# A planner's rule for TensorE's transposes, one modelled wire for two kinds of transfers, and new due times, in a hybrid attention and MLP layer

## The chip, the core and the metric

The kernel runs on one core of one Trainium2 chip. The metric is the device time of one execution in microseconds. A core has five engines that run side by side, each through its own list of instructions in order: TensorE (PE in the profile, with its weight loads apart as PEld), VectorE (DVE), ScalarE (ACT), GpSimd (POOL) and SyncE (SP, which here only starts transfers).

## The reference, cut to what matters

One layer (DEPTH = 1) on 512 tokens of width 1024, all in float32:

```python
hn = rms_norm(h, ln_mix); z = hn @ w_in
q1, q2, k1, k2, va, qf, kf, vf, fg, qc, kc, vc = split(z)
o_a = diff_attention(q1, q2, k1, k2, va, ...)   # 4 heads, two softmax maps each
o_b = forgetting_attention(qf, kf, vf, log_f)   # 6 heads, causal
o_c = chunk_attention(qc, kc, vc, rel_bias)     # 6 heads
h = h + concat(o_a, o_b, o_c) @ w_out
h = h + conv_gated_mlp(rms_norm(h, ln_ffn), w_up, conv_w, conv_b, w_down)   # d_ff = 2816
gate = sigmoid(rms_norm(h, ln_ple) @ w_ple_gate)
h = h + (p @ w_ple_proj) * gate
```

All queries and keys are normalised per head (64 wide) before the scores.

## The kernel before

Every large product is made of three passes: each operand is split into a high part (`hi`, written as fp32r) and the rest (`lo`), and `mm3` (L479) adds hi x hi, hi x lo and lo x hi into one PSUM bank. Splitting costs one ACT copy and one DVE subtraction for each tile of weights or activations (`load_w`, L407; `split`, L463). For a part of the weights the subtraction is instead done by POOL, or by a transfer that adds (`pool.dma_start` with `accum_op`, L428).

The work falls into stages. `first_products` (L584) multiplies the first eight pieces of x, k = 0 to 7, as they are loaded, with the first block of `w_in`: 8 x 12 matmuls of 384 columns. The next block is "A0b", 262 columns, whose four unit groups are called in1_0 to in1_3 (four weight tiles, made by `in_w(1)`). Then come the projections in2 to in9 (`in_unit`, `project`), the preparation of queries and keys ("A0a" and the like, `qk_cols`, L757), scores (`scores`, L846), the transposing of probabilities (`prob_cols`, L870), values (`values`, L898), and the output projection (out0, out1). Transposes run on TensorE against an identity matrix, in fp32, into one PSUM bank for four at a time (`feature_cols` L674, `prob_cols`, `split_cols` L493, `forget_cumsum` L770). 16 heads take 10 transposes of probabilities each, in three groups (kb = 0: 4, kb = 1: 3, the rest: 3). The MLP and the gate follow from L1222 on.

**The order is made by a planner.** While the program is built, the engines' calls are not issued but recorded as `Op`s in a `Plan` (L100), with what they read and write. There are two plans: the first holds all up to the end of the attention part (emitted at L1100), the second the rest (L1108 to L1944). `price` (L160) gives each operation a duration (a transpose 0.109 us, an fp32r matmul 0.0004556 us a column and 0.001), a lag, and for transfers the bytes (`move`). `due` (L201) gives each TensorE operation a due time: the sum of the durations of TensorE's operations ahead of it in program order, plus what `SHIFT` (L53) says for its group; other operations are due early enough for the ones that wait for them. A group is the name that `PLAN[-1].group` had when the operation was recorded: "in1_1", "A0s01", or at first "first". Groups that `SHIFT` does not name are not moved.

`solve` (L212) then walks through time. Again and again it takes the engine that can act first, and of the operations that are ready there the one due first (L237). On TensorE an operation counts as ready only `SURE` after its inputs (L236). For transfers it keeps two clocks, `wire["sp"]` for those from SP (0.37 MB a us) and `wire["pool"]` for those from POOL (0.105 MB a us); at most 8 of a queue are open at once (L250 to L256). The order that comes out is the order in which `emit` issues the instructions; on the chip each engine keeps to it and waits by semaphores. The planner's times are not used in any other way.

In the second plan a further list of tasks (`Task`, L1252) sets the program order of the MLP; its `dl` and `trial` are not touched.

Of the kernel before, what the change touches and what calls it, by code (L numbers as in the profile page):

```python
# [41 lines left out]
for _i in range(3):  # L42
# [5 lines left out]
AHEAD = 2  # L48
# [2 lines left out]


SHIFT = {  # L53
# [14 lines left out]
}  # L68


# [29 lines left out]
class Plan:  # L100
# [59 lines left out]
    def price(self, op):  # L160
        e, k = op.eng.name, op.k
        n = self.width(op.outs[0])
        cols = sum(1 for v in op.ins if self.width(v) == 1) - (op.name == "reciprocal")
        acc = "accum_out" in k
        op.move = 0
        if e == "pe":
            if op.name == "transpose":
                op.busy = 0.109
            else:
                op.busy = n * 0.0004556 + 0.001 if op.ins[0].dtype == F32R else n * 0.0017  # L170
            op.lag = 0.165
        elif e == "act":
            op.busy, op.lag = 0.06 + n * 0.00088 + (0.18 + 0.04 * cols if acc else 0.09 * cols), 0.1
            f = k.get("func", op.a[2] if len(op.a) > 2 else None)
            if f in (AF.Silu, AF.Sigmoid) and f not in self.loaded:
                self.loaded.add(f)
                op.busy += 1.3
        elif e == "dve":
            n = max([n] + [self.width(v) for v in op.ins])
            op.busy, op.lag = 0.07 + n * 0.001045 * (1 + (op.name == "tensor_tensor_scan")) + 0.06 * cols, 0.083  # L180
        elif op.name == "dma_start":
            op.move = n * 4 * op.outs[0].shape[0]
            op.busy, op.lag = (0.9 if e == "pool" else 0.45), 0.0
        elif op.name == "tensor_tensor":
            op.busy, op.lag = ((0.42 + n * 0.155) if k["op"] == ALU.pow else (0.1 + n * 0.0024)), 0.04
        elif op.name == "memset":
            op.busy, op.lag = 0.05 + n * 0.0009, 0.04
        else:
            op.busy, op.lag = 0.08 + n * 0.00103 + (0.12 if n > 8 else 0.2) * cols, 0.04
        op.busy *= self.SPARE.get(e, 1.0)  # L190
        here = [v for v in op.ins if v.tensor.space != bass.MemoryType.PSUM]
        op.port = e == "pool" and not op.move or e == "dve" and (
            len(here) == len(op.ins) and (op.name == "tensor_scalar" or op.name in ("tensor_tensor", "scalar_tensor_tensor")))

    LONG = 0.6
    HW, SW, AT_ONCE = 0.37e6, 0.105e6, 8
    SURE, AHEAD, MUCH, WAIT = 0.15, 1.0, 2.0, 0.6
    SPARE = {"act": 1.02, "dve": 1.02, "pool": 1.05}
    ENGINES = ("dve", "pe", "act", "pool", "sp")

# [11 lines left out]
    def solve(self):  # L212
        clock = dict(self.clock)
        free = {e: [] for e in self.ENGINES}
        for op in self.ops:
            op.left, op.at = len(op.deps), op.ready + self.LEAD[op.eng.name]
            if not op.left:
                free[op.eng.name].append(op)
        wire, out, order = {"sp": 0.0, "pool": 0.0}, {"sp": [], "pool": []}, []
        held = {"dve": 0.0, "pool": 0.0}  # L220
        other = {"dve": "pool", "pool": "dve"}
        when = lambda q: max(q.at, held[other[q.eng.name]] + (self.late if q.eng.name == "pool" else 0.0)) if q.port else q.at
# [1 line left out]
        while True:  # L224
# [8 lines left out]
            t, e = best  # L233
            can = [q for q in free[e] if when(q) <= t]
            if e == "pe":
                can = [q for q in can if q.at + self.SURE <= t] or can  # L236
            op = min(can, key=rank)  # L237
            if e not in ("pe", "sp"):
                soon = [q for q in free[e] if t < when(q) < t + op.busy * self.AHEAD and q.dl < op.dl - self.MUCH]
                if soon:  # L240
                    u = min(soon, key=rank)
                    short = [q for q in can if t + q.busy <= when(u) + 0.05]
                    if short:
                        op = min(short, key=rank)
                    elif when(u) - t < self.WAIT:
                        op = u
            free[e].remove(op)
            t0 = max(clock[e], when(op))
            busy = op.busy * (1.85 if e == "pe" and t0 < 8.6 else 1.0)
            if op.move:  # L250
                done = out[e]
                if len(done) >= self.AT_ONCE:
                    t0 = max(t0, done[-self.AT_ONCE])
                wire[e] = max(t0 + 2.0, wire[e]) + op.move / (self.HW if e == "sp" else self.SW)
                op.end = wire[e] + 0.6
                done.append(op.end)  # L256
            else:
                op.end = t0 + busy + op.lag
# [32 lines left out]
def kernel(ctx: ExitStack, tc: tile.TileContext, x, xt0, xt, pt_in, small, g_ffn_in, bias_c,  # L291
# [813 lines left out]
    for q in ("hi", "lo"):  # L1105
        pi.tile([P, 768], F32R, tag=f"w{q}", bufs=W[q])
        MORE_RAW.append(pi.again(f"w{q}", W[q], F32))
    PLAN.append(Plan(first.last, (), first.mem, first.last["dve"] + 0.6, 0.1))  # L1108

    CONV = 10  # L1110

# [106 lines left out]
    def add_h(n, j, acc):  # L1218
        for b, c in ADDS[j]:
            dve.tensor_tensor(out=hblk(b, n, c), in0=hblk(b, n, c), in1=pv(acc), op=ALU.add)  # L1220

    ple_cols()  # L1222
    for n, k in ((0, 0), (0, 1), (1, 0)):
        ple_load(n, k)
    last_out(0)
    ffn_norm(0)
    last_out(1)
    ffn_norm(1)
    last_out(2)
    ffn_norm(2)  # L1230
    for t in range(NT):
        ple_unit(0, t)
    ffn_cols(0)
    last_out(3)
    ple_load(1, 1)
    ffn_norm(3)
    ffn_cols(1)
    for t in range(2):
        ple_unit(1, t)
    mp.turn["conv"] += 2  # L1240
    for t in range(2, NT):
        ple_unit(1, t)

    SLACK, URGENT = 0.8, 3.0

# [6 lines left out]
    class Task:  # L1252


        def __init__(self, kind, parts, do, deps=(), makes=(), uses=()):
            self.kind, self.parts, self.do, self.deps = kind, parts, do, [d for d in deps if d is not None]
            self.makes, self.end, self.dl, self.next, self.after = makes, None, 1e9, [], []
            for s in (*makes, *uses):
                s.users.append(self)
            for s in uses:  # L1260
# [10 lines left out]
    COUNT = {"raw": NRAW, "hi": NHI, "conv": CONV, "pin": 1, "left": 3, "x": 3, "z": 2, "s": 2, "t": 3, "o": 1}  # L1271
    TURN = {tag: [] for tag in COUNT}
    TASKS = []


    def DV(n):
# [2 lines left out]
    def AC(n):  # L1279
        return "act", 0.2 + n * 0.00083  # L1280
# [225 lines left out]
    def up_plain(f):  # L1506
# [11 lines left out]
            return do  # L1518

        for g in range(2):  # L1520
            pe_task(36, some(g, range(6)), [more()], (), [us[g]])
            yield
        last = []
        more()
        for g in range(2):
            last.append([pe_task(12, some(g, range(6, KD)), [ws[2]], (), (), [us[g]])])
# [3 lines left out]
    def up_seven(f):  # L1530
# [5 lines left out]
        own = lambda odd, h_: [[T[(2 * i + odd) // 4][:, (2 * i + odd) % 4, h_ * H : (h_ + 1) * H] for T in (Th, Tl)] for i in range(4)]  # L1536

        def prod(o, j, right, first, deps=()):
            def do():
                if first:  # L1540
                    v[o] = bank(slots[o].tag, f"s{o}{f}")
# [51 lines left out]
    class Down:  # L1593
# [6 lines left out]
        def product(self, what, phs=None, last=True):  # L1600

            j = tuple(RIGHT).index(what)
            li, ri, an, begins = PRODUCTS[j]
            assert ri == RIGHT[what]
            for ph in phs or self.phs:
# [64 lines left out]
    def first(f, g, a):  # L1670
        def do():
# [4 lines left out]
            for k in range(KD):  # L1676
                mm3(U[c][:, cs], *first_w[f][1](g, k), Th[k // 4][:, k % 4, cs], Tl[k // 4][:, k % 4, cs], k == 0, k == KD - 1)

        if a == 0:
            us[f, g] = Slot("zs"[g])  # L1680
        return pe_task(24, do, [first_w[f][0][g], first_w[f][0][2]], FORM if a else (), [us[f, g]] if a == 0 else (), [us[f, g]] if a else ())

    def cols2(t, g):

        v, s, sm = {}, Slot("t"), Slot("pin")

        def tr():
# [97 lines left out]
    COLS3 = {}  # L1785

    def cols3(t, g):
        v, s = {}, Slot("t")

        def tr():  # L1790
# [42 lines left out]

    def gate(n, t, c0, c1):
        c = slice(n * S + c0, n * S + c1)
        v, s = {}, Slot("z")
        pps, ys = Slot("conv"), Slot("conv")

# [18 lines left out]
        for k in range(KD):  # L1857
            p = pe_task(6 * (c1 - c0) / S, lambda k=k: do(k), [wg[n][k]], [COLS3[t, g] for g in range(2)], [s] if k == 0 else (), () if k == 0 else [s])
            if (n, t) == (0, 0) and k in (2, 5):
                cols3(2 + k // 4, 1)  # L1860
        GATE_ENDS.append(Task("do", [AC(c1 - c0), DV(c1 - c0), DV(c1 - c0)], end, [p, load_, STATS[t]], [ys], [s, pps]))

    class Rest:
# [64 lines left out]
    while order:  # L1928
# [5 lines left out]
        else:  # L1934
# [4 lines left out]
            late = min((q for x, q in tr if x <= first_at + SLACK), key=lambda q: q.dl)  # L1939
            q = late if late.dl < q.dl - URGENT else q  # L1940
        _, q.end, clock = trial(q)
        q.do()
        order.remove(q)
    PLAN.pop().emit()  # L1944
# [63 lines left out]
```

## Time and profile before

| | |
|---|---|
| time, median of 3 runs | 709.53 us (709.39 to 709.59) |
| time of the profiled execution | 709.35 us |
| its span, first to last instruction | 707.2 us |
| mean granted TensorE clock | 0.998 |
| busy: PE, PEld | 698.1 us (99%), 631.3 us (89%) |
| busy: DVE, ACT, POOL | 538.4 us (76%), 392.6 us (56%), 259.5 us (37%) |
| moved | 83.22 MB, mean 118 GB/s |

The share of busy time is the time in which an engine had an instruction at work, over the span. The profile's lines name an instruction by engine, operation and "out<-in" with the program's names of tiles: `t<-ident,e` is a transpose of probabilities into a bank with tag t, `z<-whi,Th` the hi x hi pass of a projection. A line number is nearly always 325, that of the helper which issues. Rows of waits give total time, how often, and the longest; rows of the timeline give start, duration, engine and instruction, and how many of them were merged ("x4"). TensorE's matmuls overlap in the records, so that the distance from one start to the next, not the duration, is what one takes.

### The profile page before, as it was taken

How to read it: one execution, taken by the hardware profiler on the slowest of the kernel's cores; microseconds unless marked ns; L12 is line 12 of the kernel's file. 1: busy time of each engine (PE TensorE's matmuls, PEld its weight loads, DVE VectorE, ACT ScalarE, POOL GpSimd, SP SyncE). 2: the span in 40 equal slices, each digit the busy share in tenths (PEclk: the TensorE clock that was granted, in tenths of full speed). 3: DMA queues.
4: the chain of work that ended last, by engine and by line, in shares of the span. 5: the costliest groups of instructions: out<-in, count | busy, mean ns of one | idle time of the engine just before them, and what ended most of it. 6: DMA issues, size and time to landing. Idle time of an engine off the chain costs nothing.

```text
span 707.2 us, 11820 instructions
## 1 busy us (share of the span) xinstructions
PE 698.1 (99%) x4204; PEld 631.3 (89%) x4204; DVE 538.4 (76%) x1090; ACT 392.6 (56%) x745; POOL 259.5 (37%) x355
## 2 busy tenths in 40 slices
PE   7999999999999999999999999999999999999997
PEld 7999999999999888898888899889998888999886
DVE  7688899787887765879889477994689869777722
ACT  6657776675676663846564355463545444545711
POOL 3687686757664641212011142113410004353300
PEclk9999999999999999999999999999999999999999
DMA  9543553313211163745445124832263232124431
GB/s 328 201 104 91 125 136 115 104 53 105 97 46 61 61 149 108 229 148 137 162 127 145 65 90 127 201 104 63 72 193 121 87 115 79 59 66 148 143 90 52
DMA packets 36950, 83.22 MB, mean 118 GB/s; under 512 B 4214, under 2 KB 6262, under 8 KB 36892
## 3 DMA queue, kind: packets, MB, share of 16 engines
q1 hardware_dynamic: 32844, 73.52, 32.1%
q0 software_dynamic: 3760, 8.66, 6.9%
q8 instruction: 33, 0.54, 0.3%
q10 hardware_dynamic: 288, 0.30, 0.1%
q14 instruction: 25, 0.20, 0.1%
HBM read 74.19 MB, written 4.21 MB: 111 GB/s over the span
## 4 chain that ended last, share of the span: by engine, by line
PE 97%; POOL 1%; DMA 0%; DVE 0%; issue 0%; ACT 0%; POOLq 0%
PE z L325 50%; PE s L325 24%; PE t L325 15%; PE o L325 7%; DMA zn<-in_w_in_dram 0%; POOL e L325 0%; POOL rs L325 0%; POOL wlo L325 0%; DVE conv L325 0%; DVE oall L325 0%; ACT otmp L325 0%; ACT whi L325 0%; DVE zn L325 0%; ACT conv L325 0%; ACT ptc L325 0%
## 5 line engine op out<-in xcount | busy, mean ns | idle before, releaser
L325 ACT CAST whi<-wraw 128x768 fp32r<-128x768 f32 (+2 forms) x132 | 99.4, 768 | 59.0 <-PE t L325 18.1
L325 PE MATMUL z<-whi,Th 128*128 128x384 f32 (+2 forms) x356 | 123.2, 355 | 4.5 <-ACT whi L325 4.4
L325 PE MATMUL z<-wlo,Th 128*128 128x384 f32 (+2 forms) x356 | 121.9, 352 | 0.0
L325 PE MATMUL z<-whi,Tl 128*128 128x384 f32 (+2 forms) x356 | 121.6, 351 | 0.0
L325 DVE TENSOR_TENSOR wlo<-wraw,whi 128x768 fp32r<-128x768 f32 (+2 forms) x114 | 100.7, 893 | 24.9 <-ACT whi L325 24.6
L325 PEld LDWEIGHTS z<-whi,Th 128*128 128x128 f32 x356 | 67.4, 190 | 8.9 <-ACT whi L325 4.4
L325 PEld LDWEIGHTS z<-whi,Tl 128*128 128x128 f32 x356 | 67.1, 189 | 4.2
L325 PEld LDWEIGHTS z<-wlo,Th 128*128 128x128 f32 x356 | 67.2, 189 | 3.4
L325 POOL TENSOR_TENSOR wraw<-wraw,wraw 128x768 f32<-128x768 f32 (+1 forms) x14 | 23.9, 1706 | 120.8 <-DVE conv L325 75.4
L325 PE MATMUL z<-Th,whi 128*128 128x512 f32 (+1 forms) x180 | 66.3, 368 | 0.1
L325 PE MATMUL z<-Tl,whi 128*128 128x512 f32 (+1 forms) x180 | 66.2, 368 | 0.0
L325 PE MATMUL z<-Th,wlo 128*128 128x512 f32 (+1 forms) x180 | 66.1, 367 | 0.0
L325 PE MATMUL s<-Tl,whi 128*128 128x512 f32 (+1 forms) x180 | 65.1, 367 | 0.0
L325 PE MATMUL s<-Th,wlo 128*128 128x512 f32 (+1 forms) x180 | 65.0, 367 | 0.0
L325 PE MATMUL s<-Th,whi 128*128 128x512 f32 (+1 forms) x180 | 64.8, 367 | 0.0
L325 ACT ACTIVATE e<-e,st 128x128 f32<-128x128 f32 (+3 forms) x80 | 44.6, 559 | 16.6 <-DVE st L325 16.2
L325 POOL TENSOR_TENSOR rs<-rs,nhalf 128x4 f32<-128x4 f32 x40 | 43.1, 1088 | 4.9 <-DVE rs L325 1.4
L325 DVE SCALAR_TENSOR_TENSOR conv<-z,cols,conv 128x511 f32<-128x511 f32 (+1 forms) x38 | 28.4, 748 | 15.7 <-ACT conv L325 15.0
L325 PEld LDWEIGHTS s<-Th,wlo 128*128 128x128 f32 x180 | 33.8, 188 | 6.2
L325 PEld LDWEIGHTS z<-Th,whi 128*128 128x128 f32 x180 | 33.8, 188 | 6.2 <-issue 0.3
L325 PEld LDWEIGHTS s<-Tl,whi 128*128 128x128 f32 x180 | 33.8, 188 | 6.2
L325 PEld LDWEIGHTS z<-Th,wlo 128*128 128x128 f32 x180 | 33.8, 188 | 6.1
(351 smaller groups left out, 1884.1 us busy)
## 6 DMA issues: line engine op xcount, KB each, us to landing
wraw<-in_w_up_dram SPq DMA_DIRECT2D x33, 384.0 KB, 3.8
wraw<-in_w_in_dram SPq DMA_DIRECT2D x28, 384.0 KB, 3.5
wraw<-in_w_down_dram SPq DMA_DIRECT2D x17, 384.0 KB, 3.0
whi_again<-in_w_up_dram SPq DMA_DIRECT2D x12, 384.0 KB, 3.7
wraw<-in_w_out_dram SPq DMA_DIRECT2D x16, 256.0 KB, 2.8
wraw<-in_w_up_dram SPq DMA_DIRECT2D x13, 256.0 KB, 3.4
wlo<-wraw POOLq DMA_DIRECT2D x7, 384.0 KB, 4.8
wraw<-in_w_ple_gate_dram SPq DMA_DIRECT2D x10, 256.0 KB, 3.1
```

What stands on the lines that cost most here:

```text
L325: ins = getattr(self.eng, op)(*a, **k)
```

## The change

It touches the planner and its table of due times; no instruction is added to or removed from the kernel.

- `op.turns` marks transposes. On TensorE, when the most urgent ready operation is of the other kind than the last one issued, `solve` looks for ready operations of the same kind due less than `STICK` = 2.0 us later. At transposes it goes on with those. At matmuls it goes on with those if fewer than two transposes are at hand, or if the first of these matmuls is due less than 1.0 us later.
- The first matmul behind a transpose that stood alone is charged 0.08 us more in the planner's clock.
- `SURE` goes from 0.15 to 0.1.
- `wire` is one clock for transfers of both queues; the two rates stay.
- `SHIFT` is new for nearly all groups of the first plan. "first" has an entry now.
- In the second plan each group gets a name of its own (`called`, `GROUP`, and `PLAN[-1].group = q.group` where tasks are issued). `SHIFT` has an entry for none of them; its first group is called "rest" so that the entry of "first" does not reach it.

```diff
 SHIFT = {
-    "in1_1": 0.4, "in1_2": -4.5, "A0a": 0.1, "in1_3": -3.6, "in2_0": -0.9, "in2_1": 1, "A0b": 23.2, "in2_2": -4.2,
-    "A0s01": -13.3, "A0s02": -12.2, "in2_3": -2.1, "fc": 21.6, "in3_0": 3.4, "A0p0": -8.9, "A0v0": 8.1, "in3_1": -1,
...
+    "first": -11.4, "in1_0": -0.3, "in1_1": -25, "in1_2": -2.7, "A0a": -6.5, "in1_3": -12.1, "in2_0": -5.9,
+    "in2_1": 19.7, "A0b": -17.1, "in2_2": -18.9, "A0s01": -25, "A0s02": -5.9, "in2_3": -4.1, "fc": 0.8, "in3_0": 4.7,
...
-        op.move = 0
+        op.move, op.turns = 0, op.name == "transpose"
...
-    LONG = 0.6
+    LONG, STICK = 0.6, 2.0
...
-    SURE, AHEAD, MUCH, WAIT = 0.15, 1.0, 2.0, 0.6
+    SURE, AHEAD, MUCH, WAIT = 0.1, 1.0, 2.0, 0.6
...
-        wire, out, order = {"sp": 0.0, "pool": 0.0}, {"sp": [], "pool": []}, []
+        wire, out, order = 0.0, {"sp": [], "pool": []}, []
+        turns, alone = False, False
...
             op = min(can, key=rank)
+            if e == "pe" and op.turns != turns:
+                same = [q for q in can if q.turns == turns and q.dl < op.dl + self.STICK]
+                if same and (turns or sum(q.turns and q.dl < op.dl + self.STICK for q in can) < 2 or min(q.dl for q in same) < op.dl + self.STICK / 2):
+                    op = min(same, key=rank)
...
             busy = op.busy * (1.85 if e == "pe" and t0 < 8.6 else 1.0)
+            if e == "pe":
+                busy += 0.08 * (alone and not op.turns)
+                turns, alone = op.turns, op.turns and not turns
...
-                wire[e] = max(t0 + 2.0, wire[e]) + op.move / (self.HW if e == "sp" else self.SW)
-                op.end = wire[e] + 0.6
+                wire = max(t0 + 2.0, wire) + op.move / (self.HW if e == "sp" else self.SW)
+                op.end = wire + 0.6
...
     PLAN.append(Plan(first.last, (), first.mem, first.last["dve"] + 0.6, 0.1))
+    PLAN[-1].group = "rest"
...
+    def called(name, do, *a):
+        PLAN[-1].group = name
+        do(*a)
```

More of the change, by code (lines that the diff above doesn't have):

```diff
@@ L1224 @@
         ple_load(n, k)
[L1225 to L1230, printed above, removed]
+    called("last_out_0", last_out, 0)
+    called("ffn_norm_0", ffn_norm, 0)
+    called("last_out_1", last_out, 1)
+    called("ffn_norm_1", ffn_norm, 1)
+    called("last_out_2", last_out, 2)
+    called("ffn_norm_2", ffn_norm, 2)
     for t in range(NT):
-        ple_unit(0, t)
-    ffn_cols(0)
-    last_out(3)
+        called(f"ple_unit_0_{t}", ple_unit, 0, t)
+    called("ffn_cols_0", ffn_cols, 0)
+    called("last_out_3", last_out, 3)
     ple_load(1, 1)
-    ffn_norm(3)
-    ffn_cols(1)
+    called("ffn_norm_3", ffn_norm, 3)
+    called("ffn_cols_1", ffn_cols, 1)
     for t in range(2):
-        ple_unit(1, t)
+        called(f"ple_unit_1_{t}", ple_unit, 1, t)
     mp.turn["conv"] += 2
     for t in range(2, NT):
-        ple_unit(1, t)
+        called(f"ple_unit_1_{t}", ple_unit, 1, t)
     SLACK, URGENT = 0.8, 3.0
@@ L1257, in __init__ @@
             self.makes, self.end, self.dl, self.next, self.after = makes, None, 1e9, [], []
+            self.group = GROUP[0]
             for s in (*makes, *uses):
@@ L1273 @@
     TASKS = []
+    GROUP = ["first"]
     def DV(n):
@@ L1520, in up_plain @@
         for g in range(2):
+            GROUP[0] = f"u{f}_{g}"
             pe_task(36, some(g, range(6)), [more()], (), [us[g]])
@@ L1523, in up_plain @@
         last = []
+        GROUP[0] = f"u{f}_2"
         more()
@@ L1538, in prod @@
         def prod(o, j, right, first, deps=()):
+            GROUP[0] = f"s{f}_{j}"
             def do():
@@ L1602, in product @@
             j = tuple(RIGHT).index(what)
+            GROUP[0] = f"{self.name}_{what}"
             li, ri, an, begins = PRODUCTS[j]
@@ L1677, in do @@
                 mm3(U[c][:, cs], *first_w[f][1](g, k), Th[k // 4][:, k % 4, cs], Tl[k // 4][:, k % 4, cs], k == 0, k == KD - 1)
+        GROUP[0] = f"u{f}_{g}{a}"
         if a == 0:
@@ L1683, in cols2 @@
     def cols2(t, g):
+        GROUP[0] = f"x{t}{g}"
         v, s, sm = {}, Slot("t"), Slot("pin")
@@ L1787, in cols3 @@
     def cols3(t, g):
+        GROUP[0] = f"h{t}{g}"
         v, s = {}, Slot("t")
@@ L1835, in gate @@
         c = slice(n * S + c0, n * S + c1)
+        GROUP[0] = f"g{n}{t}_{c0}"
         v, s = {}, Slot("z")
@@ L1860, in gate @@
                 cols3(2 + k // 4, 1)
+                GROUP[0] = f"g00_{k}"
         GATE_ENDS.append(Task("do", [AC(c1 - c0), DV(c1 - c0), DV(c1 - c0)], end, [p, load_, STATS[t]], [ys], [s, pps]))
@@ L1941 @@
         _, q.end, clock = trial(q)
+        PLAN[-1].group = q.group
         q.do()
```

23 rows, old and new, of the table SHIFT are left out of this document.

## The prediction

> **What bounds the kernel now.** I read the page first (busy shares, chain of waits), then the windows by stage, then what TensorE's weight loads wait for, then the timeline of TensorE around its transposes.
>
> ```profile
> span 707.2 us, 11820 instructions
> PE 698.1 (99%) x4204; PEld 631.3 (89%) x4204; DVE 538.4 (76%) x1090; ACT 392.6 (56%) x745; POOL 259.5 (37%) x355
> PE 97%; POOL 1%; DMA 0%; DVE 0%; issue 0%; ACT 0%; POOLq 0%
> ```
>
> TensorE is busy 99% of the span and is 97% of the chain that ended last. The other engines matter only where TensorE stands still for them. The windows, one row a stage, say where that can be:
>
> ```profile
> 0.00:9.00 9.00, 4.62 (x15) 4.61 (x16) 4.81 (x11) 4.59 (x8) 5.80 (x15) 1.00 0.82 264
> 36.00:70.00 34.00, 33.91 (x225) 32.18 (x224) 28.75 (x90) 22.00 (x58) 27.28 (x45) 1.00 0.36 96
> 360.00:700.00 340.00, 340.00 (x2028) 300.05 (x2027) 248.83 (x354) 160.81 (x235) 75.47 (x67) 1.00 0.37 109
> 700.00:708.00 8.00, 2.98 (x25) 2.77 (x24) 1.70 (x4) 0.95 (x2) 0.00 (x0) 0.81 0.19 66
> ```
>
> The columns are stretch, length, busy time of PE, weight loads, DVE, ACT and POOL, then clock, DMA share and GB/s. TensorE starts 4.38 us into the span (4.62 busy of the first 9.00) and ends at 702.98, 4.2 us before the end. The MLP stretch, 360 to 700, is full. A busy PE hides short gaps here, because the end of a matmul is modelled and one record overlaps the next; so the gaps are read from the weight loads, which stand ahead of every matmul. All their waits between 36 and 250 us, the attention stage (total, times, longest):
>
> ```profile
> PEld s L325 <- DVE st L325: 0.9, 3, 0.4
> PEld t L325 <- DVE zn L325: 0.6, 2, 0.4
> PEld t L325 <- issue: 0.5, 2, 0.3
> PEld z L325 <- DVE zn L325: 0.4, 2, 0.2
> PEld t L325 <- ACT pth L325: 0.4, 1, 0.4
> PEld t L325 <- POOL e L325: 0.4, 1, 0.4
> PEld s L325 <- POOL k L325: 0.3, 1, 0.3
> PEld z L325 <- issue: 0.3, 1, 0.3
> PEld t L325 <- DVE ptl L325: 0.3, 1, 0.3
> PEld s L325 <- issue: 0.2, 1, 0.2
> PEld o L325 <- ACT pth L325: 0.2, 1, 0.2
> PEld o L325 <- DVE oall L325: 0.2, 1, 0.2
> PEld o L325 <- DVE ptl L325: 0.2, 1, 0.2
> ```
>
> They sum to 4.9 us in 18 waits of 0.2 to 0.4 us. From 250 us to the end the same view has one row, equal to the "z <- issue" row above: 0.3 us. Two things follow. All that a better order can win is about 4.9 + 0.3 us, 0.7% of the span. And no releaser in the list is a DMA: TensorE nowhere waits for a load once it runs.
>
> **The change part by part. First, transposes in runs.** The new planner charges 0.08 us more when one transpose stands alone between matmuls (`alone`), and keeps transposes together (`STICK`). What a lone one costs is in the timeline (start, duration):
>
> ```profile
> 102.74 0.28 PE L325 MATMUL s<-kl,q 128*128 128x256 f32 x1
> 102.85 0.28 PE L325 MATMUL s<-k,q 128*128 128x256 f32 x1
> ...
> 103.62 0.60 PE L325 MATMUL t<-ident,e 128*128 128x128 f32 x4
> 103.97 0.36 PE L325 MATMUL s<-k,q 128*128 128x256 f32 x1
> 104.18 0.27 PE L325 MATMUL t<-ident,e 128*128 128x128 f32 x1
> 104.20 0.37 PE L325 MATMUL s<-kl,q 128*128 128x256 f32 x1
> 104.41 0.27 PE L325 MATMUL t<-ident,e 128*128 128x128 f32 x1
> ```
>
> Go by starts, not durations. A 256-column matmul between matmuls takes 0.11 us (102.74 to 102.85; 0.118 is the median of its 1590 cases in the same view). The run of four with the matmul behind it takes 103.62 to 104.18, 0.56 us; less 0.118 leaves 0.44, or 0.111 a transpose. The lone one with its matmul takes 104.18 to 104.41, 0.23; less 0.118 leaves 0.112. The matmul behind a lone transpose does look 0.08 us slow (0.21 against 0.118), but it starts only 0.02 after the transpose instead of 0.11: the same time, put down to the other record. Over all runs I find 113.5 ns for a lone one, 222.6 for a pair, 441 for four: about 109 each and 4.5 a run.
>
> There are 312 transposes in 130 runs, 67 of them lone, the first and the last of these:
>
> ```profile
> 32.94 0.27 PE L325 MATMUL t<-ident,zn 128*128 128x128 f32 x1
> 307.52 0.27 PE L325 MATMUL t<-ident,conv 128*128 128x128 f32 x1
> ```
>
> If all 67 pair up, 34 runs of 4.5 ns go: 0.15 us. If they join longer runs, 67 go: 0.3 us. If none joins, nothing. By the planner's own 0.08 it would be 5.4 us, which the rows above exclude. I take **-0.15 us**.
>
> [...]
>
> ```profile
> L325 PE MATMUL t<-ident,e x160: 269/272/328, 55.6 to 265.0; 128*128 128x128 f32 x160
> 652.57 1.04 PE L325 MATMUL t<-ident,h 128*128 128x128 f32 x8
> ```
>
> **Second, where runs cost.** In `solve`, when a transpose is the most urgent ready operation and TensorE is at matmuls, it is now passed over as long as a ready matmul is due within 1.0 us behind it (within 2.0 if fewer than two transposes are at hand). Once in a run, matmuls up to 2.0 us more urgent wait for the rest of it. TensorE loses nothing itself, it only swaps. But behind a transpose come the ACT copy and the DVE subtraction of its columns, and TensorE's scores or values wait for both. In the window from 36 to 70 DVE is busy 28.75 of 34 us (85%) and POOL 27.28 (80%): a chain that starts 1 us later finds little room to catch up. Its bounds: nothing where other matmuls fill in (they did for all but 18 waits), and one more wait of 0.2 to 0.4 us for each held group. `SURE`, from 0.15 to 0.1, points the same way: operations are taken with 0.05 us less margin, at most 0.05 on each of 18 waits, 0.9 us.
>
> **Third, the due times.** Nearly every group of the attention part is moved, by up to 25 us, and "first" for the first time. This draws the order of 36 to 250 us anew. It removes no matmul and adds none, so its worth lies between all waits gone (-4.9) and, where it goes badly, a second set of the same size (+4.9). The trace shows these waits as single chains that came 0.2 to 0.4 us late with five different causes, no one cause that a new order would cure. I take **0**: about as many waits elsewhere.
>
> **Fourth, the start.** "in1_1" is moved by -25, "first" by -11.4. By the planner's prices the 96 matmuls of `first_products` run from 4.5 in steps of 0.176 to 21.4, the 24 of in1_0 to 24.3; so in1_1 is due at -0.7, and step k=4 of the first products at 4.5 - 11.4 + 4 x 2.11 = 1.5. The four loads of the A0b weights, which stood behind all x and W loads, now go out ahead of x's k=4. The rows on this:
>
> ```profile
> 4.67 0.43 SPq L325 DMA_DIRECT2D bias<-in_xt_dram  x1
> 10.12 0.33 SPq L325 DMA_DIRECT2D wraw<-in_w_in_dram  x1
> wraw<-in_w_in_dram SPq DMA_DIRECT2D x4, 262.0 KB, 5.6
> 10.13 0.73 ACT L325 ACTIVATE Th<-bias,cols 128x512 fp32r<-128x512 f32 x1 [0.58 <-DMA bias<-in_xt_dram]
> 14.95 0.63 ACT L325 CAST whi<-wraw 128x524 fp32r<-128x524 f32 x1
> 14.75 0.51 PE L325 MATMUL z<-whi,Th 128*128 128x384 f32 x2
> 15.10 0.51 PE L325 MATMUL s<-whi,Th 128*128 128x384 f32 x2
> ```
>
> Four times 262 KB is 1.07 MB; at the 264 GB/s of the first 9 us that is 4.1 us of delay for k=4 (issued now at 4.67, against 10.12 for the first A0b load). Its columns are ready at 10.86 and TensorE takes them at 14.75: 3.9 us of cover. If the four A0b splits stand ahead too (4 x 0.63 on ACT), the delay is up to 6.6, a stall of 2.7. Against that, 12 matmuls of in1_1 become ready (about 1.5 us of other work), and ACT has gaps. Bounds 0 and +2.7; I take **0**, because each later k has more cover.
>
> **Fifth, one wire.** Loads and adding transfers now share one modelled wire, so the planner holds loads for later than before. No load's issue depends on it but through the order; TensorE waits for no DMA in the list above, so earlier or later guesses have 0 to win, and a load that is put behind another costs only once its cover (the tiles split ahead) is used up. Lower bound 0, upper one more wait of 0.4; I take **0**. The names given to the MLP's groups have no entry among the due times, so they move nothing; the stretch from 360 to 700 can only lose.
>
> **Sum.** The profiled execution took 709.35 us: its span of 707.2 and 2.15 around it. 709.35 - 0.15 = **709.2 us**. The median of the runs shown, 709.53, is 0.18 above that execution, well inside what is unknown here. As "the same" I count 0.2% either side, 1.4 us (708.1 to 710.9), about what a measurement of this kernel can tell from no change.
>
> **Rivals.** (1) *The new order cures the waits.* For it: the list is all short waits, and a planner whose transfers are priced better could set chains earlier. Against it: none of them is a transfer, and the 0.08 for lone transposes makes its clock for TensorE run slower than the real one. With 45% of 4.9 gone, -2.2 and -0.15: **707.0**. Not below 704.0, with all 5.2 gone.
> (2) *Held transposes become waits.* Place: scores and values between 36 and 200 us, where DVE and POOL are over 80% busy. Price: each of the 16 heads has three groups of probability transposes; if one group in each six of these 48 ends in a further wait of 0.3, that is 8 x 0.3 = 2.4, with 0.3 for `SURE`: **711.9**. It decides once a held transpose has no more than about 1 us of matmuls of another group behind it.
> (3) *The start stalls*, as worked out: +2.7, **711.9**. It decides if the columns of k=4 are split after about 16.2 us (14.75 and the 1.5 of in1_1).
> [...]
>
> **How the numbers follow.** Forecast 46%; rival 1 30%; rival 2 16%; rival 3 6%; rival 4 1%; a stall in the MLP stretch past 1.4 us 1%. So faster 0.30, the same 0.46, slower 0.24. The forecast's own range is 708.1 to 710.9. For 8 in 10 I reach to rivals 1 and 2 with 0.2 to 0.3 beyond them: 706.8 to 712.2, leaving out the best third of rival 1 and the worst of 2 and 3.
>
> **What would show it.** Merging: far fewer single transposes in TensorE's timeline, yet matmul spacing behind a run still near 0.21, and a lone one still 0.112. Due times: the sum of the weight loads' waits between 36 and 250; 4 to 6 us means the forecast, under 3.5 rival 1, over 6.5 rival 2, then with "ACT pth", "DVE ptl" or "DVE st" as releasers. Start: A0b loads issued before x's fifth piece; a gap in TensorE before 23 us is rival 3. Wrong I am if the MLP stretch stops being full, or if the tail after the last matmul leaves 4.2 us.

## The result, and the profile after

The changed kernel takes 712.94 us (median of 6 runs, 712.46 to 713.40) beside 709.58 for the kernel before (6 runs, 709.39 to 710.30): a ratio of 1.0046 [1.0034, 1.0058]. It is **slower by 3.4 us** (2.4 to 4.1 by the interval). The forecast was 709.2 in a range of 706.8 to 712.2; it was wrong.

The profiled execution of the changed kernel took 713.28 us. Its page:

```profile
span 711.5 us, 11852 instructions
PE 698.7 (98%) x4204; PEld 632.1 (89%) x4204; DVE 537.8 (76%) x1090; ACT 394.1 (55%) x745; POOL 264.0 (37%) x355
PE 94%; DVE 2%; POOL 1%; ACT 1%; issue 0%; DMA 0%; ACTq 0%; POOLq 0%
```

TensorE's work is what it was. What grew is the chain's share that is not TensorE: 97% before, now 94%, and DVE, at 0% before, has joined the chain with 2%. The windows show the place (columns as in the prediction: stretch, length, busy time of PE, weight loads, DVE, ACT and POOL, clock, DMA share, GB/s). Before:

```profile
120.00:140.00 20.00, 19.80 (x120) 19.09 (x119) 16.12 (x59) 13.21 (x33) 15.05 (x22) 1.00 0.37 105
140.00:165.00 25.00, 24.94 (x152) 22.99 (x151) 20.62 (x68) 18.27 (x44) 14.68 (x24) 1.00 0.17 47
```

After:

```profile
120.00:140.00 20.00, 17.89 (x112) 16.37 (x110) 16.93 (x55) 12.27 (x27) 16.23 (x24) 1.00 0.36 97
140.00:165.00 25.00, 23.94 (x145) 22.73 (x146) 19.73 (x71) 15.36 (x39) 13.54 (x20) 1.00 0.39 118
360.00:700.00 340.00, 340.00 (x2018) 299.50 (x2017) 251.24 (x356) 162.25 (x237) 74.81 (x67) 1.00 0.36 109
```

TensorE is idle for 2.9 us more in these 45 us. The MLP stretch is as full as before and the clock is 1.00. All waits of the weight loads between 36 and 250 us, the view that the prediction rests on (total, times, longest):

```profile
PEld s L332 <- POOL k L332: 3.0, 3, 1.5
PEld s L332 <- DVE st L332: 1.8, 3, 1.4
PEld t L332 <- issue: 0.9, 3, 0.4
PEld t L332 <- DVE ptl L332: 0.5, 1, 0.5
PEld o L332 <- DVE ptl L332: 0.5, 2, 0.3
PEld s L332 <- issue: 0.4, 1, 0.4
PEld z L332 <- DVE wlo L332: 0.4, 1, 0.4
PEld t L332 <- DVE zn L332: 0.3, 1, 0.3
PEld o L332 <- issue: 0.3, 1, 0.3
PEld t L332 <- DVE st L332: 0.2, 1, 0.2
PEld z L332 <- DVE V L332: 0.2, 1, 0.2
```

The sum went from 4.9 to 8.5 us, and the count stayed at 18. So it is not more waits, but **longer** ones: before none was longer than 0.4, now one took 1.5 and one 1.4. The first two rows hold all of the loss.

What happened there is in the timelines of DVE, POOL and TensorE (start, duration; rows picked out, other rows lie between them). Around 123 us in the changed kernel:

```profile
122.05 0.62 POOL L332 TENSOR_SCALAR k<-k 64x512 fp32r<-64x512 f32 x1
122.28 0.73 DVE L332 SCALAR_TENSOR_TENSOR kl<-t,cols,k 64x512 fp32r<-64x512 f32 x1
122.75 2.00 POOL L332 TENSOR_SCALAR q<-ql 64x512 fp32r<-64x512 f32 x1
123.33 0.94 DVE L332 TENSOR_TENSOR wlo<-wraw,whi 128x768 fp32r<-128x768 f32 x1
123.73 0.38 PE L332 MATMUL t<-ident,zn 128*128 128x128 f32 x2
124.72 0.61 POOL L332 TENSOR_SCALAR k<-k 64x512 fp32r<-64x512 f32 x1
125.39 0.39 PE L332 MATMUL s<-k,q 128*128 128x256 f32 x1 [1.27 <-POOL k L332]
```

POOL moves the halves of queries and keys to their places, 0.61 us a move. The second one took 2.00: before its 0.61 were over, DVE began a weight subtraction (`wlo<-wraw,whi`). The move ends at 124.75, 0.48 after the subtraction's end at 124.27. Only then comes the move of k on which the scores wait: TensorE stands still for 1.5 us. Nothing was in a hurry for that subtraction; by the planner's due times its weights are wanted 25 us later.

Around 157 us it is DVE that loses:

```profile
156.02 3.90 DVE L332 TENSOR_TENSOR wlo<-wraw,whi 128x768 fp32r<-128x768 f32 x2
156.96 2.13 POOL L332 TENSOR_TENSOR wlo<-wraw,whi 128x768 fp32r<-128x768 f32 x1
158.79 0.40 PE L332 MATMUL o<-pth,V 128*128 128x512 f32 x1
159.84 0.34 DVE L332 CUSTOM_DVE_ANT_0 e<-s,fbias,st 128x128 f32<-128x128 f32 x1
160.24 0.50 PE L332 MATMUL s<-k,q 128*128 128x512 f32 x1 [1.06 <-DVE st L332]
```

Two subtractions, 0.95 us each elsewhere, take 3.90 together (the first row is both, merged); POOL's own subtraction of a third tile, 156.96 to 159.09, ran beside the second, which ended 0.83 after it. The exponentials behind them (159.84) come late, and TensorE waits 1.2 us. The third place, around 50 us, is like the first:

```profile
49.99 1.35 POOL L332 TENSOR_SCALAR k<-k 64x512 fp32r<-64x512 f32 x1
50.20 0.66 DVE L332 TENSOR_TENSOR wlo<-wraw,whi 128x512 fp32r<-128x512 f32 x1
51.39 0.39 PE L332 MATMUL s<-k,q 128*128 128x256 f32 x1 [0.41 <-POOL k L332]
```

TensorE's gaps at the three places are 1.51, 1.22 and 0.58 us, 3.3 together: the size of the loss. The planner assumes that such instructions exclude each other: `op.port` (L192 of the kernel before) marks them, and `held` in `solve` (L222) lets a marked one begin only when the other engine's is over. But `emit` (L280) puts this on the chip as a wait only in the second plan (`self.late`). In the first plan the order of each engine is all that is left of it, and as soon as one engine runs ahead of or behind the planner's clock, an instruction planned behind another lands beside it.

**Theory:** three unguarded collisions of DVE and POOL are the loss (theory A in the expectations). **Rivals:** the transposes in runs come too late (the prediction's second rival, theory B); or the new due times are a worse order at large, with the collisions as a symptom.

### The profile page after: what moved, and what is told of

It is laid out like the page before. It is cut to its first block, busy times and chain, and to the rows that moved or that the text cites. A ratio compares the mean times of both kernels' runs of the same rounds, so it can differ in the third digit from the quotient of the medians.

```text
span 711.5 us, 11852 instructions
## 1 busy us (share of the span) xinstructions
PE 698.7 (98%) x4204; PEld 632.1 (89%) x4204; DVE 537.8 (76%) x1090; ACT 394.1 (55%) x745; POOL 264.0 (37%) x355
## 4 chain that ended last, share of the span: by engine, by line
PE 94%; DVE 2%; POOL 1%; ACT 1%; issue 0%; DMA 0%; ACTq 0%; POOLq 0%
PE z L332 48%; PE s L332 24%; PE t L332 15%; PE o L332 7%; POOL k L332 1%; POOL q L332 1%; DVE wlo L332 1%; DMA zn<-in_w_in_dram 0%; DVE e L332 0%; ACT e L332 0%; POOL rs L332 0%; DVE kl L332 0%; DVE oall L332 0%; ACT whi L332 0%; DVE bias L332 0%
## 5 line engine op out<-in xcount | busy, mean ns | idle before, releaser
L332 PE MATMUL z<-wlo,Th 128*128 128x384 f32 (+2 forms) x356 | 123.4, 351 | 0.0
L332 DVE TENSOR_TENSOR wlo<-wraw,whi 128x768 fp32r<-128x768 f32 (+2 forms) x114 | 102.8, 911 | 24.4 <-ACT whi L332 23.9
L332 DVE CUSTOM_DVE_ANT_0 e<-s,bias 128x128 f32<-128x128 f32 (+3 forms) x74 | 33.7, 469 | 12.9 <-PE s L332 7.2
L332 DVE TENSOR_TENSOR conv<-conv,conv 128x512 f32<-128x512 f32 (+1 forms) x31 | 20.8, 678 | 25.5 <-ACT conv L332 25.4
```

What stands on the lines that cost most here:

```text
L332: ins = getattr(self.eng, op)(*a, **k)
```

## The experiments

Each run stands beside runs of the kernel before on the same chip: 709.92, 709.84 and 709.88 us in the three sets.

**Three waits, order untouched.** To the changed kernel, three waits are added that hold the chip to the planner's own order at the three places (a mapping from the held instruction's number to the one it waits for). `g2` has only the one for 123 us, `g3` only that for 157.

```diff
+    EDGES = {586: 441, 1676: 1221, 1956: 1953}
...
+            if not self.late and op.pos in self.EDGES:
+                op.eng.behind(op.ins, self.ops[self.EDGES[op.pos]].ins)
```

> The changed kernel with its order untouched and three waits added: DVE's subtraction for a weight tile of in2_3 waits for POOL's move of a key tile of A0b, the one of the fifth weight tile issued with group A1n waits for POOL's move of the last key tile of B0a, and POOL's subtraction of the third weight tile of in7_3 waits for DVE's of the second. Theory A (DVE and POOL instructions that overlap hold each other up, and three such meetings stand ahead of TensorE's waits of 0.58, 1.51 and 1.22 us): about 3.3 us come back, 709.6 to 710.4 against 712.9 for the changed kernel. Theory B (transposes held by the new rule come late): the order of TensorE is the same, so 712.5 to 713.4.

> The changed kernel with the second of the three waits alone (DVE's weight subtraction behind POOL's move of the last key tile of B0a). Theory A: 1.5 us back, 711.2 to 711.7, the wait of TensorE near 124 us gone and the one near 159 us left. Theory B: 712.5 to 713.4.

> The changed kernel with the third of the three waits alone (POOL's weight subtraction behind DVE's). Theory A: 1.2 us back, 711.5 to 712.0, the wait near 159 us gone and the one near 124 us left. Theory B: 712.5 to 713.4.

All three: 709.58 (708.63 to 709.94), ratio 0.9992 [0.9983, 1.0001]. The one at 123: 711.83, 1.0028 [1.0018, 1.0038]. The one at 157: 711.50, 1.0023 [1.0014, 1.0032]. Against the 1.0046 of the changed kernel that is 3.8, 1.3 and 1.6 us won, each to about 1 us either way by the intervals; the rest of the 3.8, about 0.9, is left for the third place, whose wait was not run alone. Where a place has no added wait, TensorE's gap comes again: 1.21 and 0.57 us at the two others with the one for 123, 1.51 and 0.58 with the one for 157. Three waits in 11,852 instructions give the whole loss back, with the new order, the runs of transposes and the one wire all in place. The two longest waits of TensorE are gone from its list (three waits added):

```profile
PEld s L336 <- POOL k L336: 0.7, 1, 0.7
...
PEld s L336 <- DVE st L336: 0.4, 2, 0.2
```

In the timeline around 123 us the subtraction now waits for the move of k, and the queries' move behind it takes the delay, where nobody is waiting:

```profile
121.83 0.73 DVE L336 SCALAR_TENSOR_TENSOR kl<-t,cols,k 64x512 fp32r<-64x512 f32 x1
122.30 0.61 POOL L336 TENSOR_SCALAR q<-ql 64x512 fp32r<-64x512 f32 x1
122.88 0.61 POOL L336 TENSOR_SCALAR k<-k 64x512 fp32r<-64x512 f32 x1
123.53 0.96 DVE L336 TENSOR_TENSOR wlo<-wraw,whi 128x768 fp32r<-128x768 f32 x1 [0.57 <-POOL k L336]
123.57 1.39 POOL L336 TENSOR_SCALAR q<-ql 64x512 fp32r<-64x512 f32 x1
```

That refutes "a worse order at large" as the source of the loss, and the late transposes with it: the order is the same, and the transposes stand in the same 66 runs. It shows too that a collision need not cost anything (the last two rows are one); it costs where TensorE waits for the loser.

**A wait at every alternation.** In the first plan every marked instruction over 0.25 us, or behind one, waits for the marked one ahead of it on the other engine.

```diff
-                if before and op.eng.name == "pool" and before.eng.name == "dve" and op.busy > self.LONG and self.late:
+                if before and op.eng.name != before.eng.name and (op.eng.name == "pool" and op.busy > self.LONG if self.late else max(op.busy, before.busy) > 0.25):
```

> The changed kernel, order untouched, with a wait wherever in the first plan one of DVE and POOL follows the other at an instruction that the planner counts as using what the two share, and one of the two is longer than 0.25 us: the planner's order between them is enforced. Theory A: all such meetings go, 708.5 to 709.8; if each added wait costs its engine 0.1 us and the engines have no room, up to 711. Theory B: 712.9 or more, since waits are only added.

711.90, ratio 1.0029 [1.0017, 1.0040]: a miss for the theory in its simple form. The long collisions are gone (none of POOL's moves of 64x512 takes over 0.70 us), but TensorE has other stalls: about 0.7 us near 47 and 0.44 near 170, which the three waits alone don't have, and 0.83 near 139 where they have 0.56. Holding an engine to the planner's order everywhere costs 2.3 us (by the medians, 2.6 by the ratios) against holding it at three places.

**The transposes out of their runs.** Three waits as in the first, and TensorE's transposes set in turn with matmuls: in `k1` wherever the data allow, in `k2` only with matmuls whose inputs are planned ready 0.5 us earlier, and no transpose moved by 0.6 us or more.

```diff
+    def alternate(self, order):
...
+            if order[pe[a]].turns and order[pe[a - 1]].turns:
...
+                    if not m.turns and all(at[d] < pe[a] for d in m.deps) and all(at[q] > pe[b] for q in t.next):
+                        order[pe[a]], order[pe[b]] = m, t
```

> The kernel with the three added waits, its order changed on TensorE alone and only inside the first plan: wherever two transposes stand side by side, a matmul that is ready by then changes places with the second. 134 transposes then stand alone in place of 3, in 179 runs in place of 66. By the new planner's price, 0.08 us for each lone one, 131 x 0.08 = 10.5 us more: 720. By the trace of the kernel before, 4.5 ns for each further run, 113 x 4.5 ns = 0.5 us, and some waits of 0.1 to 0.3 us where the last transpose of a bank comes later: 710.0 to 711.5.

> As the run before that set transposes and matmuls in turn, on the kernel with the three added waits, but a matmul changes places with a transpose only if by the plan its inputs from other engines are there 0.5 us before, and the transpose moves back by less than 0.6 us. 85 transposes stand alone in place of 3, in 140 runs in place of 66. By 0.08 us for each lone one: 82 x 0.08 = 6.6 us more than 709.6, 716. By 4.5 ns a run: 74 x 4.5 ns = 0.3 us, 709.9, and up to 711 where a later last transpose of a bank is waited for.

`k1` has 134 lone transposes in 179 runs and takes 715.39, ratio 1.0078 [1.0066, 1.0091]. It fits neither expectation, and it doesn't answer the question cleanly: by the distances of starts, TensorE's own work is only about 0.5 us more, while the waits grew, by matmuls put ahead of their inputs and by banks whose last transpose comes later (first rows of its weight loads' waits):

```profile
PEld s L350 <- DVE st L350: 2.6, 7, 0.7
PEld o L350 <- ACT pth L350: 1.2, 3, 0.6
```

`k2` has 85 lone ones in 140 runs and takes 711.03, ratio 1.0014 [1.0005, 1.0023], 1.5 us more than the first experiment. TensorE's work is 0.3 to 0.4 us more, which is 74 runs more (140 against 66) at 4 to 5 ns, near the prediction's 4.5; a lone one takes about 113 ns. By the planner's 0.08 the 82 lone ones more would be 6.6 us. The rest, some 1.1 us, are waits again:

```profile
PEld o L350 <- DVE ptl L350: 1.0, 4, 0.3
```

So in this order taking the runs apart costs 1.5 us, mostly in such waits and little in TensorE's own work, and the second rival, in which the runs do the harm, falls. That merging helps in general isn't shown: the kernel before, planned with 67 lone transposes, takes as long as the changed one with its three waits.

**Rules and due times apart.** `f3` is the changed kernel without `STICK` and the 0.08; `f1` is the kernel before with the new `SHIFT` table alone (and the group "rest").

> The changed kernel with the rule for transposes and the 0.08 us taken out of the planner, all else as changed. If the rule makes the loss, the time goes down towards 709.6. If the due times fit only the rules they were drawn for, the order falls apart: the planner itself then reckons with 21 us more, so 725 to 735.

> The planner of the kernel before, all its rules, with the new due times alone. If the due times alone make the loss, about 712.9. If rules and due times fit only together, far slower: this planner reckons with 23 us more, so 725 to 740.

736.69 and 736.32 us, one run each: 24 and 23 us more than the changed kernel. The table belongs to its rules, and the planner itself reckoned such a loss (21 and 23 us). What either is worth alone can't be read from this. It does show how far an order reaches: the same instructions, 24 us apart.

**The same cure on the kernel before.** Two waits at collisions near 131 and 162 us of the kernel before.

```diff
+    EDGES = {1679: 1295, 1672: 1564}
```

> The kernel before with two waits added, order untouched: DVE's subtraction of the sixth weight tile issued with A1n waits for POOL's 4-column scaling of in5_3, and DVE's step of the normalisation of A1 waits for POOL's scaling of a block of probabilities of B1. Both pairs overlap in its trace, 1.08 us in place of 0.27 and 0.88 in place of 0.37, ahead of TensorE's waits of 0.36 near 131 us and 0.22 near 162. If meetings of DVE and POOL are at work in the kernel before too, 0.3 to 0.6 us less, 709.0 to 709.4 against 709.6; if they are a matter of the new due times alone, no change.

709.28, ratio 0.9992 [0.9983, 1.0001]: in time not told from nothing. In the trace both waits of TensorE are gone (0.36 to 0.03 and 0.22 to nothing). One of them in the timelines, first before, with the subtraction beside it:

```profile
127.74 1.08 POOL L325 TENSOR_SCALAR rs<-rs,rstd 128x4 f32<-128x4 f32 x1 [0.35 <-DVE rs L325]
127.82 0.95 DVE L325 TENSOR_TENSOR wlo<-wraw,whi 128x768 fp32r<-128x768 f32 x1
```

and with the two waits:

```profile
128.34 0.27 POOL L329 TENSOR_SCALAR rs<-rs,rstd 128x4 f32<-128x4 f32 x1 [0.34 <-DVE rs L329]
```

So the kernel before had such collisions too, small ones where TensorE waited for them.

**A fourth wait.** The three, and POOL's move of a query near 131 us behind four small DVE instructions that had stood in its way.

```diff
-    EDGES = {586: 441, 1676: 1221, 1956: 1953}
+    EDGES = {586: 441, 1676: 1221, 1956: 1953, 1425: 1336}
```

> The kernel with the three added waits and a fourth: POOL's move of a query tile of B1a waits for the last of four small DVE instructions of B0's scores, with which it overlaps at 130.4 to 131.8 us (DVE took 1.22 us for the four). If this meeting too holds up the chain to TensorE's waits of 0.41 near 134 us and 0.56 near 137, 0.3 to 0.8 us less than 709.6; if POOL's own queue is what is late there, no change or up to 0.5 more.

708.99 (708.68 to 709.50), ratio 0.9988 [0.9979, 0.9997]: **faster than both kernels**, by 0.9 us (0.2 to 1.5 by the interval) than the one before, and by some 4 us than the changed one. What the fourth wait adds to the three isn't shown: the two intervals overlap, 0.9988 and 0.9992, and by the gaps between TensorE's matmuls the wait near 134 (0.41 us) is gone while the one near 137 grew from 0.56 to 0.86, 0.1 us won in all. The weight loads' waits between 120 and 140 us are down to two rows:

```profile
PEld s L336 <- POOL k L336: 1.0, 1, 1.0
PEld s L336 <- issue: 0.4, 1, 0.4
```

With the three waits there is a third, `t <- issue` with 0.5.

## Why the prediction was wrong

**Merging (-0.15, at most -0.3): right.** 130 runs became 66, the lone transposes 67 became 3, and TensorE's work by the distances of starts fell by some 0.2 us. The 0.08 that the planner charges isn't in the trace, before or after.

**Held transposes and `SURE` (bounded by one more wait a group): no harm seen.** With the three waits the transposes stand in the same runs, and the time is that of the kernel before. No run tests `SURE` alone. The second rival's premise was half right: in the windows of the profile before, DVE is over 80% busy from 36 to 200 us, but POOL only 80% from 36 to 70, and 63 to 70% after that.

**Due times (0, between -4.9 and +4.9): this is the step that failed.** It took "about as many waits elsewhere", and in number that is what came, 18 and 18. They sum to 8.5 us instead of 4.9, so the term measured +3.6. The mistake was the unit. "Waits of 0.2 to 0.4 us" were taken for what a wait in this kernel costs, and the second rival was priced with it (8 times 0.3). But those were the waits of an order that, by luck or by the fit of its due times, had only small ones of the collisions in TensorE's way; a collision on the chain to the scores costs 0.6 to 1.5. With that unit, three waits fill the whole bound: 3.3 of 4.9. The prediction also called the 18 waits chains "with five different causes, no one cause". Its rows name seven tiles of three engines, and what releases a wait isn't yet its cause: the two waits that `b1` removes were put down to DVE's zn and POOL's e, and both came of a collision.

What the prediction could have seen: the order is only as good as the planner's clock, and the planner has a rule (`op.port`, `held`) that the chip isn't held to in the first plan. It was not asked what becomes of it in a new order. Groups of one form show it as a spread of their mean; POOL's moves of queries in the changed kernel (busy time and mean ns of one):

```profile
L332 POOL TENSOR_SCALAR q<-ql 64x512 fp32r<-64x512 f32 x20 | 15.0, 749 | 1.7 <-POOL q L332 0.2
```

The same row before:

```profile
L325 POOL TENSOR_SCALAR q<-ql 64x512 fp32r<-64x512 f32 x20 | 13.1, 657 | 1.9 <-DVE ql L325 0.4 <-POOL q L325 0.2
```

One alone takes 0.61 us, so even the 657 told of collisions in a kernel whose order was about to be changed. The view tells where to look and not what it costs: over all of POOL's forms in the first 280 us the time beyond each form's median is the same in both kernels, about 16 us. What differs is who waits for it.

**Start (0, at most +2.7): right.** Three of the four A0b loads, not all four, go out ahead of x's k = 4 (`bias`), the fourth behind k = 5 (SyncE's timeline after; in the kernel before, k = 4 went out at 4.67):

```profile
3.95 0.33 SPq L332 DMA_DIRECT2D wraw<-in_w_in_dram  x1
...
4.80 0.44 SPq L332 DMA_DIRECT2D wraw<-in_w_in_dram  x1
...
5.77 0.44 SPq L332 DMA_DIRECT2D wraw<-in_w_in_dram  x1
6.26 1.13 SPq L332 DMA_DIRECT2D bias<-in_xt_dram  x2
7.43 0.68 SPq L332 DMA_DIRECT2D wraw<-in_w_in_dram  x1
```

No wait for them came of it. The first 36 us are 0.7 us slower in the profiled execution, of which most is 17 matmuls at the slow pace of the start (0.32 us from one to the next, 0.17 later) instead of 13, a number that went from 12 to 17 among the profiles of this case. The granted clock reads 1.00 there too, so that column doesn't tell the slow pace.

**One wire (0): right.** No transfer is among the releasers. **MLP: right**: the stretch is full, though the tail behind the last matmul is 4.5 us instead of 4.2. No run shows the term behind the 1% of rival 4, matmuls slowed by long runs of transposes: behind the changed kernel's runs of up to 12 the matmuls go on, from the second one and where they wait for nothing, at their usual distance, 0.17 to 0.18 us for 384 columns and 0.23 to 0.24 for 512, and the granted clock of 360 to 700 reads 1.00 as before.

The prediction's test, "over 6.5 us means rival 2", did fire (8.5), and the 711.9 of rivals 2 and 3 is the nearest number in it; yet neither mechanism came. Of the releasers named for rival 2, "DVE st" did come, second with 1.8 us, but the timeline near 157 puts its long wait down to a subtraction held up by POOL, not to a transpose held back; the first row is POOL, which was not named. The range failed with the same step: its term reached to +4.9, 714 us, but the upper end was set by the rival at 711.9 and 0.3 beyond.

Open: how much of the loss is due to the rule and how much to the due times, since one falls apart without the other; what `SURE` and the one wire are worth alone; and whether the planner, without its 0.08, would find a better order.

## What to carry to other kernels

When an order is made by a model, list what the model assumes and the chip doesn't enforce; a new order draws these anew, and the waits of the old one say nothing of their size. Look for instructions that take far longer than the rest of their form, see what ran beside them on the other engine, and put a wait only where somebody on the critical path waits for the loser: here three waits gave back 3.8 us, and waits everywhere gave up 2.3 of these again.

## What the runs showed of the hardware

By the recorded times DVE and POOL didn't slow each other by a share, one stood still for the other. In the twelve profiles of this case POOL's moves of 64x512 occur 720 times. 51 took over 0.70 us, and 48 of these end 0.47 to 0.49 after the end of a DVE instruction whose tensor operands all lie in SBUF, such as `wlo<-wraw,whi`, whatever its length. In the profiles of the kernel before and the changed one it is 9 of 120, and all nine end 0.48 after one, of 0.66 to 1.41 us. In their other overlaps the move took 0.61 to 0.66, and DVE's subtraction of 768 columns, begun up to 0.34 us into it, took 1.08 to 1.42 instead of 0.95 and ended 0.80 to 0.81 after the move. Beside `kl<-t,cols,k`, which takes one operand from PSUM, and no other DVE instruction, some 100 moves took 612 to 627 ns; the 122.30 row of the three waits is one. The three of the 120 with no DVE instruction beside them took 611 to 612.

Who loses can't be told from the starts in a profile: POOL's move began 0.58 us ahead in the 122.75 row and 0.21 ahead in the 49.99 row and lost both. What decides it, and what the two share, was not measured here beyond these times.
